# Cosine-similarity attention on one core: a five-bank score ring with exponentials of two and three banks, and the norms moved out of their PSUM bank

## The chip, the cores and the metric

One core of a Trainium2 chip. The metric is the device time of one launch in microseconds (us). The kernel before takes 189.99 us (median of 3 runs, 189.53 to 190.36).

## The reference

Q, K and V are [8, 12, 512, 64] in f32, tau is 0.1.

```python
Q_norm = Q / (np.linalg.norm(Q, axis=-1, keepdims=True) + 1e-10)
K_norm = K / (np.linalg.norm(K, axis=-1, keepdims=True) + 1e-10)
scores = np.einsum('bhqd,bhkd->bhqk', Q_norm, K_norm) / tau
weights = np.exp(scores - np.max(scores, axis=-1, keepdims=True))
weights = weights / (np.sum(weights, axis=-1, keepdims=True) + 1e-10)
return np.einsum('bhqk,bhkd->bhqd', weights, V).astype(np.float32)
```

There are 96 heads. For each, 512 x 512 exponentials are taken. The kernel leaves out the maximum: a cosine over tau lies between -10 and 10.

## The kernel before

**The work.** Two heads make a pair; there are 48 pairs, s = 0 to 47. All five engines run in order, each through its own list, and the lists are written out by hand in `ORDER` (numbers of operations in the order in which they are added). A step waits on semaphores for what it needs (`needs`), so a step whose input is late holds up all that stands behind it on its engine. The steps of one pair, with their names in the code, engines and lines:

- Q, K and V arrive by DMA (SP's queue). `SQ`: POOL squares Q and K together (L350).
- `SSQ`: for K, eight matmuls with the identity on PE add up the squares to eight columns a row, in columns 320 to 383 of an output bank `ops` (L367); `RED`: DVE adds up the rest (L375). For Q, DVE reduces the squares itself (L379).
- `NEW`: one over the root of the sums for a group of pairs (single pairs at first, then twos, from pair 20 on fours), eight or nine short DVE steps, each of which needs the one before it (L404 to L413).
- `SCL`: Q is scaled by DVE, K by POOL, in nine pairs by DVE (L437). `TR`: eight transposes on PE (L443), `EVA`: DVE copies them to `qt` (L451), a ring of four pairs.
- `SCO`: scores, 512 keys by 512 queries of a head; a chunk c is 128 keys of both heads, two matmuls of 512 columns into two PSUM banks (L550). `EXP`: ACT takes the exponential of the chunk, 1024 columns, to `et` (L566), a ring of five pairs.
- `PV`: for each head (h = 0 or 1) 16 matmuls of 65 columns on output bank `ops` h (L583); column 65 of each holds the sum of the weights. `RCP` (L594) and `NRM` (L596): DVE divides, and SP stores.

**PSUM** has eight banks: four for the scores (`scps`: chunk after chunk takes banks 0 and 1, then 2 and 3, in turn), two for the outputs (`ops0`, `ops1`), one for the transposes (`tps`), one for the norms (`nps`: the sums of squares, the Newton steps' product and the finished factors). A score chunk can be written when the exponential two chunks earlier has read its banks:

```python
used = [("EXP", 0, 2 * c, 1)] if turn < NT + 2 else exps(*chunks[turn - 2])
P.add(("SCO", s, c), "pe", "sco", T0 + 0.9 * c, used + [("EVA", s)], sco)
```

A `PV` of one output bank can start when `NRM` of the pair before has read that bank (`bank_free`).

**Around the loop.** Pair 0 has its own head (`head0`), with `FILL` matmuls on PE that compute nothing used. In pair 43 one chunk's exponential is made by DVE and POOL with a polynomial (`OFF`). The last pair ends in pieces (`last`).

Of the kernel before, what the change touches and what calls it, by code (L numbers as in the profile page):

```python
# [10 lines left out]
class Op:  # L11
    def __init__(self, key, eng, kind, due, needs, emit, slot=None):
# [3 lines left out]
        self.gate = None  # L16
# [4 lines left out]
class Program:  # L21


    def __init__(self, nc):
        self.nc, self.ops, self.list = nc, {}, []
# [18 lines left out]
    def run(self):  # L44
# [68 lines left out]
def bass_cosine_similarity_attention_kernel(  # L113
# [26 lines left out]
    et = [sb(f"et{i}", [128, NT, 2, SEQ], bf16) for i in range(R_ET)]  # L140
# [13 lines left out]
    sc_ps = nc.alloc_psum_tensor("scps", [128, 4, SEQ], f32)  # L154
# [4 lines left out]
    n_ps = nc.alloc_psum_tensor("nps", [128, R_X, 160], f32)  # L159
# [70 lines left out]
    for s in range(NP):  # L230
        for h in range(2):
            bank_free[s, h] = before[h]
            before[h] = [("NRM", s, h)] + ([("RED",) + attached[s, h]] if (s, h) in attached else [])

# [75 lines left out]
    def pair(s):  # L310
# [47 lines left out]
        x2 = (xs[g][:, 0 : 2 * m] if acts else n_ps[:, g % R_X, 0 : 2 * m]).rearrange("p (w x) -> p w x", w=2)  # L358
# [26 lines left out]
        rkd = n_ps[:, g % R_X, 128 + m : 128 + 2 * m] if acts else tg[:, m : 2 * m]  # L385
        on_dve = [i for i in range(first[g], first[g] + sizes[g]) if i in K_ON_DVE]
# [16 lines left out]
        elif s == first[g]:  # L403
# [13 lines left out]
            if on_dve:  # L417
                steps.append(up(tg[:, m : 2 * m], m, 2 * m))
            for k, step in enumerate(steps):
                needs = [("NEW", g, min(k, 6) - 1 if k < 8 else 7)] if k else reds + (free[1] if K_ON_DVE else [])  # L420
                if k == 0 and g == R_X:
                    needs += [("NRMS", 0, w, h) for w in range(2) for h in range(2)]
                if 6 <= k < 8:
                    needs += free[k - 6]
                P.add(("NEW", g, k), "dve", "new", TF - 4.9 - slack(s, M_NEW) + (M_STEP * (k - 7) if s > 8 else 0.23 * k), needs, step)

        if s in off_of:
            P.add(("UNIT", s), "dve", "new", TF - 3.0, [("NEW", g, 6)], lambda e: e.tensor_scalar(
                out=rq_g[:, c8 : c8 + 8], in0=rq_g[:, c8 : c8 + 8], scalar1=UNIT * inv_tau / math.log(2.0), scalar2=1.0,
                op0=ALU.mult, op1=ALU.mult))  # L430
        for w in range(2):
# [3 lines left out]
            P.add(("SCL", s, w), "dve" if dve else "pool", "sclq" if dve else "sclk", T0 - (2.85 if w and not dve else 2.55) - slack(s, M_SCL),  # L435
# [3 lines left out]
                      in0=qk[iq][:, w].rearrange("p h (t d) -> p h t d", t=NT), in1=r, op=ALU.mult))  # L439

# [15 lines left out]
    def scos(s):  # L456
        if s < 0:
            return []
        if s in off_of:
            return [("SCO", s, c) if c != off_of[s] else ("SCX", s, c - c) for c in range(NT)] + [("SCX", s, 1)]  # L460
        return [("SCO", s, c) for c in range(NT)] if s else [("SCO", 0, c, h) for c in range(NT) for h in range(2)]
# [4 lines left out]
    def exps(s, c):  # L466
# [6 lines left out]
        return [("Y", s, last_step(s, c)) if (s, c) in OFF else ("EXP", s, c)]  # L473
# [46 lines left out]
    def rest(s):  # L520
# [3 lines left out]
        for c in range(NT):  # L524
# [20 lines left out]
            turn = chunks.index((s, c))  # L545
            b = turn % 2

            def sco(e, c=c, b=b):
                for h in range(2):
                    last = e.matmul(  # L550
                        out=sc_ps[:, 2 * b + h, :], lhsT=qt[iqt][64 * h : 64 * h + 64, 1, c, :],
                        rhs=qt[iqt][64 * h : 64 * h + 64, 0, :, :], start=True, stop=True)
                return last

            used = [("EXP", 0, 2 * c, 1)] if turn < NT + 2 else exps(*chunks[turn - 2])
            P.add(("SCO", s, c), "pe", "sco", T0 + 0.9 * c, used + [("EVA", s)], sco)
            if last_pair and c == NT - 1:
# [90 lines left out]
UNIT = 128.0  # L648
# [167 lines left out]
```

## Time and profile before

| | |
|---|---|
| runs | 189.99 us median of 3, 189.53 to 190.36 |
| profiled execution | 190.25 us, of which the span from the first to the last instruction is 188.4 us |
| granted TensorE clock | 0.998 |
| busy share of the span | PE 93%, DVE 91%, ACT 96%, POOL 86% |
| instructions | PE 2714, DVE 552, ACT 213, POOL 150 |

How to read it: the profile is one execution. A busy time is the union of an engine's instructions, so overlapping ones count once; the mean of one instruction can therefore be longer than the step from one to the next. Idle time is put down to what ended it. The chain is followed back from the last instruction to what released each piece.

### The profile page before, as it was taken

Reading aid. Unit: us, or ns where it says so; the run is one execution under the profiler, and the core shown is the slowest. Engines: PE = TensorE matmul, PEld = TensorE weight load, DVE = VectorE, ACT = ScalarE, POOL = GpSimd, SP = SyncE. Lnnn points to the kernel's source line nnn. Section 1 sums busy time; section 2 is a strip of 40 time slices with the busy share of each in tenths; the row PEclk is TensorE's granted clock in tenths of the full one; section 3 lists DMA queues with packets and bytes.
Section 4 is the critical chain, followed back from the end, with each engine's and each line's share of the span. In section 5 each row is a group of like instructions: output and inputs, shape, how many; then the busy total and the mean of one; then the engine's idle time right before and its main releaser. Section 6 shows DMA issues by size and latency. Waiting matters only on the chain.

```text
span 188.4 us, 6686 instructions
## 1 busy us (share of the span) xinstructions
PE 174.7 (93%) x2714; PEld 108.8 (58%) x2714; DVE 170.5 (91%) x552; ACT 181.8 (96%) x213; POOL 162.1 (86%) x150
## 2 busy tenths in 40 slices
PE   7998998999999999999989999999989999999993
PEld 2555664666566566566656666666655555565662
DVE  2789999999999999999999998999999999998663
ACT  4799999999999999999999999999999999999993
POOL 5799999999999999999999999899999990594500
PEclk9999999999999999999999999999999999999999
DMA  5999999999999699999999869999470800038058
GB/s 164 348 353 351 349 350 282 294 377 378 379 366 356 188 293 347 377 381 361 366 373 354 285 187 336 380 361 349 123 234 5 278 6 0 3 120 273 2 179 270
DMA packets 52446, 50.76 MB, mean 269 GB/s; under 512 B 3136, under 2 KB 52416, under 8 KB 52416
## 3 DMA queue, kind: packets, MB, share of 16 engines
q1 hardware_dynamic: 51984, 50.02, 80.4%
q8 instruction: 21, 0.34, 0.7%
q10 hardware_dynamic: 432, 0.33, 0.5%
q14 instruction: 9, 0.07, 0.1%
HBM read 37.75 MB, written 12.58 MB: 267 GB/s over the span
## 4 chain that ended last, share of the span: by engine, by line
ACT 92%; PE 5%; DVE 1%; issue 0%; POOL 0%; POOLq 0%
ACT et L566 90%; PE ops L195 2%; PE ops L198 1%; DVE qn L437 1%; ACT et L542 1%; PE scps L533 1%; ACT et L561 0%; PE ops L281 0%; ACT ob L627 0%; PE ops L367 0%; DVE qt L292 0%; DVE ob L631 0%; PE tps L443 0%; PE scps L550 0%; PE tps L281 0%
## 5 line engine op out<-in xcount | busy, mean ns | idle before, releaser
L566 ACT ACTIVATE et<-scps 128x1024 bf16<-128x1024 f32 x186 | 170.6, 1203 | 0.0
L350 POOL TENSOR_TENSOR sq<-qk 128x1024 bf16<-128x1024 f32 x44 | 82.7, 1894 | 0.3 <-DMA qk<-in_Q_dram 0.3
L550 PE MATMUL scps<-qt 64*128 64x512 bf16 x374 | 73.0, 387 | 8.9 <-ACT et L566 6.4
L583 PE MATMUL ops<-vb,et 128*128 128x65 bf16 x1504 | 75.7, 194 | 0.0
L583 PEld LDWEIGHTS ops<-vb,et 128*128 128x128 bf16 x1504 | 56.7, 98 | 29.2 <-issue 18.8
L437 POOL TENSOR_TENSOR qn<-qk,rk 128x512 bf16<-128x512 f32 x38 | 39.2, 1043 | 1.9 <-DVE rk L409 1.5
L596 DVE TENSOR_TENSOR ob<-ops,rd 128x256 f32<-128x256 f32 x94 | 38.9, 418 | 0.8
L437 DVE TENSOR_TENSOR qn<-qk,nps 128x512 bf16<-128x512 f32 x56 | 37.0, 678 | 0.5 <-ACT nps L396 0.5
L550 PEld LDWEIGHTS scps<-qt 64*128 64x128 bf16 x374 | 18.1, 93 | 27.8 <-ACT et L566 17.9
L443 PE MATMUL tps<-ident,qn 128*128 128x128 bf16 x376 | 33.9, 220 | 0.1
L451 DVE COPY qt<-tps 128x1024 bf16<-128x1024 bf16 x47 | 32.1, 684 | 1.4 <-PE tps L443 1.2
L571 POOL TENSOR_SCALAR vb<-vf 128x512 bf16<-128x512 f32 x48 | 29.4, 627 | 2.6 <-DVE et L499 2.6
L379 DVE TENSOR_REDUCE nps<-sq 128x8 f32<-128x512 bf16 x46 | 31.2, 682 | 0.0
L443 PEld LDWEIGHTS tps<-ident,qn 128*128 128x128 bf16 x376 | 21.6, 98 | 9.4 <-issue 6.1
L594 DVE RECIPROCAL rd<-ops 128x4 f32<-128x4 f32 x94 | 16.0, 175 | 5.3 <-PE ops L583 4.3
L367 PE MATMUL ops<-sq,ident 128*128 128x64 bf16 x384 | 18.8, 193 | 0.0
L367 PEld LDWEIGHTS ops<-sq,ident 128*128 128x128 bf16 x384 | 14.3, 98 | 3.4 <-issue 2.2
L375 DVE TENSOR_REDUCE nps<-ops 128x8 f32<-128x64 f32 x46 | 10.0, 219 | 0.7 <-PE ops L367 0.4
L499 POOL TENSOR_TENSOR xz<-xz 128x1024 f32<-128x1024 f32 x1 | 1.9, 1892 | 6.6 <-DVE xz L494 6.6
L405 DVE SCALAR_TENSOR_TENSOR nps<-nps,ys 128x32 f32<-128x32 f32 (+2 forms) x34 | 7.0, 207 | 0.4
L404 DVE TENSOR_TENSOR nps<-nps,ys 128x32 f32<-128x32 f32 (+2 forms) x34 | 7.0, 205 | 0.4
L344 POOL TENSOR_TENSOR sq<-qk 128x512 bf16<-128x512 f32 (+1 forms) x5 | 4.6, 954 | 0.3 <-DMA qk<-in_K_dram 0.2
(67 smaller groups left out, 63.5 us busy)
## 6 DMA issues: line engine op xcount, KB each, us to landing
vf<-in_V_dram SPq DMA_DIRECT2D x48, 256.0 KB, 5.9
qk<-in_Q_dram SPq DMA_DIRECT2D x47, 256.0 KB, 6.1
qk<-in_K_dram SPq DMA_DIRECT2D x47, 256.0 KB, 6.1
out_dram<-ob SPq DMA_DIRECT2D x47, 256.0 KB, 5.4
qk<-in_Q_dram SPq DMA_DIRECT2D x2, 128.0 KB, 2.6
qk<-in_K_dram ACTq DMA_DIRECT2D x2, 128.0 KB, 2.8
out_dram<-ob SPq DMA_DIRECT2D x1, 128.0 KB, 2.0
out_dram<-ob SPq DMA_DIRECT2D x1, 64.0 KB, 1.8
```

Source lines behind the costliest of these rows:

```text
L350: lambda e: e.tensor_tensor(out=sqf, in0=data, in1=data, op=ALU.mult))
L367: last = e.matmul(out=o_ps[bank][:, 320:384], lhsT=ident[:, :], rhs=sq[iqs][:, 8 * w : 8 * w + 8, 8 * k : 8 * k + 8], start=(k == 0), stop ...
L379: lambda e, w=w, dst=dst: e.tensor_reduce(out=dst, in_=sq[iqs][:, 8 * w : 8 * w + 8, :], axis=AX.X, op=ALU.add))
L437: lambda e, w=w, r=r: e.tensor_tensor(out=qn[iqn][:, w].rearrange("p t h d -> p h t d"), in0=qk[iq][:, w].rearrange("p h (t d) -> p h t d" ...
L443: last = e.transpose(t_ps[:, w, t, :], qn[iqn][:, w, t].rearrange("p h d -> p (h d)"), ident[:, :])
L451: lambda e: e.tensor_copy(out=qt[iqt][:, :, :, :].rearrange("p w t x -> p (w t x)"), in_=t_ps[:, :, :, :].rearrange("p w t x -> p (w t x)")))
L550: last = e.matmul(out=sc_ps[:, 2 * b + h, :], lhsT=qt[iqt][64 * h : 64 * h + 64, 1, c, :], rhs=qt[iqt][64 * h : 64 * h + 64, 0, :, :], sta ...
L566: lambda e, c=c, b=b: e.activation(out=et[iet][:, c, :, :], in_=sc_ps[:, 2 * b : 2 * b + 2, :], func=ACT.Exp, scale=math.log(2.0) / UNIT i ...
L571: lambda e: e.tensor_scalar(out=vb[:, iq, :, :, 0:DIM].rearrange("p c h d -> p h c d"), in0=vf[iv][:, :, :].rearrange("p h (c d) -> p h c ...
L583: last = e.matmul(out=o_ps[h][:, 65 * t : 65 * t + 65], lhsT=et[iet][:, c, h, 128 * t : 128 * t + 128], rhs=vb[:, iq, c, h, :], start=(c = ...
L594: lambda e, h=h, grid=grid: e.reciprocal(out=rd[io][:, h, :], in_=grid[:, :, DIM]))
L596: lambda e, h=h, grid=grid: e.tensor_tensor(out=ob[io][:, h], in0=grid[:, :, 0:DIM], in1=rd[io][:, h, :].unsqueeze(2).to_broadcast([128, N ...
```

## The change

From pair 12 on (`WIDE`) the norms leave their PSUM bank and that bank becomes a fifth bank of `scps`. Score units (one bank: one head of one chunk) are taken two at a time into banks 0 and 1, then three at a time into banks 2, 3 and 4, in turn, and each group of units has one exponential, of 1024 or 1536 columns. `et` becomes one tile, so that such a group may run over a chunk's end or a pair's end; where the ring of `et` wraps, at pair 43 and before the last chunk the groups are cut. The list of ACT then has 103 exponentials of 1024 columns, 55 of 1536 and one of 512, where there were 186 of 1024; the columns are the same 190,464. DVE has 552 instructions as before.

The sums of squares of those pairs go to SBUF (`xn`), the Newton product to SBUF (`ys`), and the running root and the finished factors to columns 384 and up of an output bank, `ops0` or `ops1` by the group's number. `run()` therefore adds waits: a group's first Newton step waits for a `RCP` on that bank, and each first `PV` of a bank waits for the last DVE step on that bank's norm columns that stands ahead of that `PV`'s `RCP` in DVE's list. For pairs under 12 the norms stay where they were (the bank has another name, so order rows call it `scps`). A first triple that takes the bank waits for the last scalings that read it. `PV` now waits for the exponentials of its own head alone.

All lists in `ORDER` are written anew, the head's too. In the rows below, names are as in the code, numbers behind a name are the buffer; a row with `x7` is seven like instructions.

PE at the start of the program; before, `ops1<-warm_in` up to 512 columns are warm-up and fills, `ops0<-ident,qn0` are transposes of pair 0's K, `tps<-ident,qn0` of its Q:

```order
L195 MATMUL ops1<-warm_in,ident 128x512 x7
L198 MATMUL ops1<-warm_in,ident 128x384
L198 MATMUL ops1<-warm_in,ident 128x128
L198 MATMUL ops1<-warm_in,ident 128x192
L198 MATMUL ops1<-warm_in,ident 128x384
L281 MATMUL ops0<-ident,qn0 64x128 [waits s_act]
L281 MATMUL ops0<-ident,qn0 64x128 x3
L198 MATMUL ops1<-warm_in,ident 128x192
L281 MATMUL tps<-ident,qn0 64x128 [waits s_dve]
L281 MATMUL tps<-ident,qn0 64x128 x3
```

and now:

```order
L203 MATMUL ops1<-warm_in,ident 128x512 x7
L206 MATMUL ops1<-warm_in,ident 128x256
L206 MATMUL ops1<-warm_in,ident 128x192
L353 MATMUL ops0<-ident,qn0 64x128 [waits s_act]
L353 MATMUL ops0<-ident,qn0 64x128 x3
L353 MATMUL tps<-ident,qn0 64x128 [waits s_dve]
L353 MATMUL tps<-ident,qn0 64x128 x3
L206 MATMUL ops1<-warm_in,ident 128x384 x2
L206 MATMUL ops1<-warm_in,ident 128x128
```

Fills of 1280 columns stood ahead of the transposes of Q, and now 448 stand there; the rest comes behind.

PE while it makes the scores of pairs 18 and 19 (`scps<-qt2`, `qt3`); `ops0<-vb,et2` is the first `PV` of pair 17, `ops0<-sq0` an `SSQ`, `ops1<-vb,et1` `PV` of pair 16. Before:

```order
L550 MATMUL scps<-qt2 128x512 [waits s_act]
L550 MATMUL scps<-qt2 128x512
L443 MATMUL tps<-ident,qn3 128x128 [waits s_dve]
L443 MATMUL tps<-ident,qn3 128x128 x3
L583 MATMUL ops0<-vb,et2 128x65 [waits s_pool,s_dve]
L583 MATMUL ops0<-vb,et2 128x65 x3
L550 MATMUL scps<-qt2 128x512 [waits s_act]
L550 MATMUL scps<-qt2 128x512
L583 MATMUL ops0<-vb,et2 128x65 x12
L367 MATMUL ops0<-sq0,ident 128x64 x8
L550 MATMUL scps<-qt3 128x512 [waits s_dve,s_act]
L550 MATMUL scps<-qt3 128x512
```

and now, with the same `PV` of pair 17 and the same `SSQ`:

```order
L286 MATMUL scps<-qt2 128x512 [waits s_act]
L286 MATMUL scps<-qt2 128x512 x2
L658 MATMUL ops0<-vb,et 128x65 [waits s_dve]
L658 MATMUL ops0<-vb,et 128x65 x15
L440 MATMUL ops0<-sq0,ident 128x64 [waits s_pool]
L440 MATMUL ops0<-sq0,ident 128x64 x7
L286 MATMUL scps<-qt2 128x512 [waits s_act]
L286 MATMUL scps<-qt2 128x512
L658 MATMUL ops1<-vb,et 128x65 [waits s_dve]
L658 MATMUL ops1<-vb,et 128x65 x7
L286 MATMUL scps<-qt3 128x512 [waits s_act]
L286 MATMUL scps<-qt3 128x512 x2
```

Scores come as three banks and two in turn, and all 16 `PV` matmuls of the head and the eight of `SSQ` stand in one piece between a triple and a double.

DVE at the norms of pairs 20 to 23, while pairs 15 to 17 are divided (`rd` 7, 0 and 1 belong to pairs 15, 16 and 17). Before:

```order
L594 RECIPROCAL rd0<-ops0 128x4 [waits s_pe]
L375 TENSOR_REDUCE nps<-ops0 128x8
L413 TENSOR_SCALAR ys0<-nps 128x64 [waits s_dve]
L404 TENSOR_TENSOR nps<-nps,ys0 128x64 [waits s_dve]
L596 TENSOR_TENSOR ob0<-ops0,rd0 128x256 [waits d_out0]
L405 SCALAR_TENSOR_TENSOR nps<-nps,ys0 128x64 [waits s_dve]
L409 SCALAR_TENSOR_TENSOR ys0<-nps,ys0 128x64 [waits s_dve]
L594 RECIPROCAL rd7<-ops1 128x4 [waits s_pe]
L404 TENSOR_TENSOR nps<-nps,ys0 128x64 [waits s_dve]
L451 COPY qt3<-tps 128x1024 [waits s_pe]
```

and now:

```order
L490 TENSOR_SCALAR ops0<-xn0 128x64 [waits s_dve]
L481 TENSOR_TENSOR ys0<-xn0,ops0 128x64 [waits s_dve]
L482 SCALAR_TENSOR_TENSOR ys0<-ys0,ops0 128x64 [waits s_dve]
L673 TENSOR_TENSOR ob0<-ops0,rd0 128x256 [waits d_out0]
L486 SCALAR_TENSOR_TENSOR ops0<-ys0,ops0 128x64 [waits s_dve]
L671 RECIPROCAL rd7<-ops1 128x4 [waits s_pe]
L481 TENSOR_TENSOR ys0<-xn0,ops0 128x64 [waits s_dve]
L482 SCALAR_TENSOR_TENSOR ys0<-ys0,ops0 128x64 [waits s_dve]
L536 COPY qt3<-tps 128x1024
L673 TENSOR_TENSOR ob7<-ops1,rd7 128x256
L671 RECIPROCAL rd1<-ops0 128x4 [waits s_pe]
L486 SCALAR_TENSOR_TENSOR rk0<-ys0,ops0 128x32 [waits s_dve]
```

The Newton steps now work in `ops0`. The `PV` of pair 17 on `ops0` waited for `ob0<-ops0` alone; it now waits for the second `L482`, and the `RCP` that needs it (`rd1<-ops0`) stands two DVE instructions behind that.

The diff, cut to its core:

```diff
+        behind = {}
+        for o in order["dve"]:
+            if o.bank is not None:
+                behind[o.bank] = o.key
+            if o.key[0] == "RCP" and o.key[2] in behind:
+                self.first_value[o.key[1:]].needs.insert(0, behind.pop(o.key[2]))
...
-    et = [sb(f"et{i}", [128, NT, 2, SEQ], bf16) for i in range(R_ET)]
+    et_all = sb("et", [128, R_ET * NT * 2, SEQ], bf16)
...
-    sc_ps = nc.alloc_psum_tensor("scps", [128, 4, SEQ], f32)
+    sc_ps = nc.alloc_psum_tensor("scps", [128, 5, SEQ], f32)
+    xn = [sb(f"xn{i}", [128, 64], f32) for i in range(3)]
...
-    n_ps = nc.alloc_psum_tensor("nps", [128, R_X, 160], f32)
+    n_ps = sc_ps[:, 4, 0 : R_X * 160].rearrange("p (r x) -> p r x", r=R_X)
...
+    while units:
+        banks = [2, 3, 4] if side else [0, 1]
+        side = 1 - side
...
+        while len(take) < min(len(banks), len(units)):
+            v = units[len(take)]
+            if place(v) != place(take[-1]) + 1 or (v[0] in off_of) != (u[0] in off_of) or (v[:2] == (NP - 1, NT - 1)) != ends:
+                break
+            take.append(v)
...
+        plan.append((*keys, take, banks, sorted({bank_last[b] for b in banks if bank_last[b]}, key=str)))
...
+            for (s, c, h), b in zip(us, banks):
+                last = e.matmul(
+                    out=sc_ps[:, b, :], lhsT=qt[s % R_QT][64 * h : 64 * h + 64, 1, c, :],
+                    rhs=qt[s % R_QT][64 * h : 64 * h + 64, 0, :, :], start=True, stop=True)
...
+                   lambda e: e.activation(
+                       out=et_all[:, i : i + len(us), :], in_=sc_ps[:, banks[0] : banks[0] + len(us), :],
+                       func=ACT.Exp, scale=math.log(2.0) / UNIT if s in off_of else inv_tau))
...
+        inner = first[g] >= WIDE
...
+        if inner:
+            n_bank = o_ps[g % 2]
+            xg, tg, yg = xn[g % 3][:, 0 : 2 * m], ys[g % R_X][:, 0 : 2 * m], n_bank[:, 384 : 384 + 2 * m]
+            rq_g, rkd = n_bank[:, 448 : 448 + m], n_bank[:, 480 : 480 + m]
...
+                if k == 0 and inner:
+                    needs += [("RCP", 0, g % 2)] + (new(g - 2) if before2 else [])
...
+WIDE = 12
```

More of the change, by code (lines that the diff above doesn't have):

```diff
@@ new lines, in bass_cosine_similarity_attention_kernel @@
+    bank_last[4] = None
+    units = [(s, c, h) for s in range(WIDE, NP) for c in range(NT) for h in range(2) if (s, c) not in OFF]
+    place = lambda u: ((u[0] % R_ET) * NT + u[1]) * 2 + u[2]
+    side = 0
+    while units:
+        banks = [2, 3, 4] if side else [0, 1]
+        side = 1 - side
+        u = units[0]
+        take = [u]
+        ends = u[:2] == (NP - 1, NT - 1)
+        while len(take) < min(len(banks), len(units)):
+            v = units[len(take)]
+            if place(v) != place(take[-1]) + 1 or (v[0] in off_of) != (u[0] in off_of) or (v[:2] == (NP - 1, NT - 1)) != ends:
+                break
+            take.append(v)
+        units = units[len(take):]
+        banks = banks[: len(take)]
+        n = len(plan)
+        keys = (("SCO", NP - 1, NT - 1), None) if ends else (("SCG", n), ("EXG", n))
+        for v in take:
+            sc_of[v], ex_of[v] = keys
+        plan.append((*keys, take, banks, sorted({bank_last[b] for b in banks if bank_last[b]}, key=str)))
+        for b in banks:
+            bank_last[b] = keys[1]
@@ L544, in rest @@
                 continue
[L545 to L557, printed above, removed]
+            if s >= WIDE and not (last_pair and c == NT - 1):
+                continue
+            n = next(n for n, p in enumerate(plan) if (s, c, 0) in p[2])
+            banks = wide(n)
+            if s >= WIDE:
                 for k, (h, lo, hi) in enumerate(PIECES):
```

90 lines of the change are left out of this document (65 added, 25 removed), and 146 rows, old and new, of the table ORDER.

## The prediction

> **What bounds the kernel now.** I read the page's busy shares and chain first, to see which engine sets the end.
>
> ```profile
> PE 174.7 (93%) x2714; PEld 108.8 (58%) x2714; DVE 170.5 (91%) x552; ACT 181.8 (96%) x213; POOL 162.1 (86%) x150
> ACT 92%; PE 5%; DVE 1%; issue 0%; POOL 0%; POOLq 0%
> ```
>
> The chain in order of time says where ACT holds it:
>
> ```profile
> 13.32 170.20 ACT et L566 x186
> 183.53 0.89 ACT et L561
> ```
>
> From 13.32 to 183.53 us nothing but the 186 exponentials is on the chain: 170.20 / 186 = 0.915 us each (170.6 / 186 = 0.917 by busy time, below). Ahead of it lies a head of 13.3 us, behind it 4.9 us of the last pair. Next the windows, to see whether ACT ever waits and how much the others have left:
>
> ```profile
> core 0: us, PE busy (x) PEld busy (x) DVE busy (x) ACT busy (x) POOL busy (x), PEclk, DMA share, GB/s
> 50.00:70.00 20.00, 19.34 (x317) 12.28 (x313) 19.50 (x71) 20.00 (x24) 19.97 (x16) 1.00 0.94 308
> 70.00:90.00 20.00, 19.16 (x314) 12.02 (x310) 19.20 (x60) 20.00 (x23) 19.97 (x19) 1.00 1.08 365
> 90.00:110.00 20.00, 19.21 (x322) 12.59 (x320) 19.38 (x65) 20.00 (x23) 19.40 (x18) 1.00 0.94 316
> 110.00:130.00 20.00, 19.10 (x318) 12.32 (x316) 18.90 (x56) 20.00 (x23) 19.47 (x19) 1.00 1.05 347
> 130.00:150.00 20.00, 18.69 (x298) 11.73 (x296) 19.60 (x65) 20.00 (x23) 19.80 (x17) 1.00 0.55 174
> ```
>
> ACT never waits: 20.00 of 20.00 everywhere. But DVE is idle for only 0.50 + 0.80 + 0.62 + 1.10 + 0.40 = 3.42 us in these 100 us. A pair is four exponentials, 3.67 us, so DVE has 0.125 us to spare per pair. So the kernel is ACT's, with DVE close behind.
>
> **The change part by part. The exponentials.** What does one of them cost beside its columns? The groups by shape:
>
> ```profile
> L566 ACT ACTIVATE et<-scps 128x1024 bf16<-128x1024 f32 x186 | 170.6, 1203 | 0.0
> L542 ACT ACTIVATE et<-scps,xs 128x512 bf16<-128x512 f32 x4 | 2.5, 680 | 0.6 <-PE scps L533 0.6
> L538 ACT ACTIVATE et<-scps 128x1024 bf16<-128x1024 f32 x2 | 2.0, 1024 | 0.2 <-PE scps L533 0.2
> L342 ACT ACTIVATE sq<-qk 128x512 bf16<-128x512 f32 x1 | 0.6, 614 | 0.0
> L342 ACT ACTIVATE sq<-qk 128x256 bf16<-128x256 f32 x1 | 0.4, 400 | 0.0
> ```
>
> The two squares give the column rate: (614 - 400) / 256 = 0.836 ns, so 1024 columns are 0.856 us and the step of 0.917 us holds 0.061 us that does not depend on the columns. The columns stay 190,464; the instructions go from 186 to 103 + 55 + 1 = 159. 27 x 0.061 = **1.65 us less**, all of it on the path as long as ACT never waits. No row shows three banks read by one instruction, so this has bounds. An exponential after a wait takes 1.024 us (L538), 0.168 us over its columns: if all of that were saved it would be 27 x 0.168 = 4.5 us, but the step of 0.917 shows that 0.107 of it overlaps already. On the other side, the 0.061 could belong to the step from one bank to the next: 186 such steps before, 103 + 2 x 55 = 213 now, which is 1.65 us more. Against that speaks L542, one bank only, with more than 0.061 over its columns. I take 1.65.
>
> The Trainium skill (ScalarE: Activation LUTs, What ACT_TABLE_LOAD costs) gives 186 ns + 0.833 ns a column for such an instruction, and an overlap of about 93 ns between neighbours, so 93 ns are left of each; 27 x 0.093 would be 2.5 us. The trace's 0.917 us for 1024 columns is below the 0.946 us that follows from this, so I go by the row.
>
> **The five-bank ring.** Two timeline pieces show when scores must be ready:
>
> ```profile
> 93.78 2.15 ACT L566 ACTIVATE et<-scps 128x1024 bf16<-128x1024 f32 x2
> 95.06 0.39 PE L550 MATMUL scps<-qt 64*128 64x512 bf16 x2 [0.52 <-ACT et L566]
> ...
> 26.00 3.93 ACT L566 ACTIVATE et<-scps 128x1024 bf16<-128x1024 f32 x4
> 26.32 0.39 PE L550 MATMUL scps<-qt 64*128 64x512 bf16 x2 [0.20 <-ACT et L566]
> 26.64 0.67 PE L583 MATMUL ops<-vb,et 128*128 128x65 bf16 x16
> 27.14 0.40 PE L367 MATMUL ops<-sq,ident 128*128 128x64 bf16 x8
> 27.47 0.39 PE L550 MATMUL scps<-qt 64*128 64x512 bf16 x2
> ...
> 7.60 0.60 PE L533 MATMUL scps<-qt 64*128 64x512 bf16 x2
> ```
>
> The first two exponentials end at 95.93 and, one step of 0.917 earlier, at 95.01; PE stood waiting and began 0.05 us behind. In the second piece exponentials end at 29.93, 29.01, 28.10 and 27.18; the chunk at 27.47 came 0.29 us after its banks were free, was done at 27.86, 0.24 us ahead of 28.10, and ACT lost nothing. So a lead of 0.24 is harmless, and with it a pair of banks may start 0.29 us late. The pair's two matmuls run beside each other in 0.39. A third has to share rows with one of them; in L533 the second of two such ends 0.60 us after the first began, 0.21 later. A triple is thus done 0.05 + 0.60 = 0.65 us after its banks are free, while the exponential of 1024 runs 0.917: a lead of 0.27, so it may be late by 0.03 us only. A double has the 1536 exponential (1.28 + 0.06 = 1.34 us) beside it and may be late by 1.34 - 0.24 - 0.44 = 0.66.
>
> Does PE reach each triple in time? A cycle of five banks is 0.92 + 1.34 = 2.26 us.
>
> ```profile
> PEld scps L550 <- ACT et L566: 17.9, 61, 0.8
> PEld ops L583 <- DVE ob L596: 3.1, 12, 0.5
> ```
>
> Its weight loads for scores waited 17.9 us for ACT over 170 us, 0.24 us in 2.26. At pairs 17 to 19 (order above) PE has, behind the triple, 16 `PV` and 8 `SSQ`: the same work in the second piece takes 26.64 to 27.47, 0.83 us. With the triple itself (0.32 for two, from 26.32 to 26.64, and 0.21 for the third) PE is at the double 0.05 + 0.53 + 0.83 = 1.41 after the triple's banks were free, the double's banks having been free since 0.92: 0.49 late of 0.66, so it fits. Then a double (0.32) and eight `PV` and it is at the next triple by about 2.0 of 2.26. So the lists work if inputs are on time. PE's waits for DVE, 3.1 us in 12 places up to 0.5, pass on to ACT where they stand ahead of a triple. Nothing if none do; all 55 triples late like the chunk at 27.47 would be 55 x (0.29 - 0.05 - 0.03) = 11.6 us. The rows are nearer to the first end, since PE has 0.24 a cycle to catch up. A triple that runs into the next pair also needs `EVA` up to two banks earlier:
>
> ```profile
> 96.06 0.69 DVE L451 COPY qt<-tps 128x1024 bf16<-128x1024 bf16 x1
> 97.10 0.39 PE L550 MATMUL scps<-qt 64*128 64x512 bf16 x2
> ```
>
> Here the copy ends 0.35 us ahead of its first use, less than a bank's 0.46; a stall for that happens once, since it moves all that follows. For both I take **0.5 us more**.
>
> **The norms.** DVE keeps its 552 instructions, of like shapes, each still with one operand in PSUM; writing `xn` or `ys` where it wrote `nps` I cost at nothing, within 27 steps of 0.01 us either way. What is added is a wait. In `PV` of pair 17 the first matmul now waits for the second `L482`, and behind it on PE stand the other 15, `SSQ` and the double; the `RCP` that needs them has only these as cover:
>
> ```profile
> L596 DVE TENSOR_TENSOR ob<-ops,rd 128x256 f32<-128x256 f32 x94 | 38.9, 418 | 0.8
> L451 DVE COPY qt<-tps 128x1024 bf16<-128x1024 bf16 x47 | 32.1, 684 | 1.4 <-PE tps L443 1.2
> ```
>
> 1.10 us of cover against 0.50 + 0.40 = 0.90 for `PV` and `SSQ` by the second piece, and 0.05 for each of two handovers: DVE waits for 0 if PE stands ready, and up to 0.53 if a triple is ahead of it. Groups from pair 12 on are four of two and seven of four: 11, so 0 to 5.8 us of DVE's time at one such place each. ACT's gain takes 1.65 / 36 = 0.046 us per pair from DVE's 0.125, and 0.079 x 36 = 2.8 us stay as cover. I take it that they do.
>
> The Trainium skill (PSUM — Partial Sum Buffer, PSUM bank collisions raise a hardware error) says that PSUM must be guarded by bank, since two engines on different columns of one bank collide too; it speaks against norms in an output bank, and is why these waits can't be left out. No run here shows a collision.
>
> **The head.** These rows lie on its way:
>
> ```profile
> 4.76 0.40 ACT L247 ACTIVATE qn<-qk 128x256 bf16<-128x256 f32 x1
> 5.25 0.41 DVE L270 TENSOR_TENSOR qn<-qk,scps 128x256 bf16<-128x256 f32 x1
> 6.68 0.41 PE L281 MATMUL tps<-ident,qn 128*64 128x128 bf16 x4
> 6.78 4.76 POOL L344 TENSOR_TENSOR sq<-qk 128x256 bf16<-128x256 f32 x5 [0.18 <-DMA qk<-in_K_dram]
> 8.24 1.27 ACT L542 ACTIVATE et<-scps,xs 128x512 bf16<-128x512 f32 x2 [0.58 <-PE scps L533]
> 12.06 0.68 DVE L451 COPY qt<-tps 128x1024 bf16<-128x1024 bf16 x1
> ```
>
> Q is scaled by 5.66, yet its transposes begin at 6.68: fills stand ahead, and most now come behind. That could bring the first exponential forward from 8.24 to about 7.7, where ACT ends its squares. But POOL starts pair 1's squares when K lands, at 6.78, which no list moves, and `EVA` of pair 1 ends at 12.74 on a DVE that is full from there on. Between -0.5 and +0.2, which is a late Q scaling, I take **-0.2 us**.
>
> **Sum.** 190.25 (the profiled execution: span 188.4, 1.85 around it) - 1.65 + 0.5 - 0.2 = 188.9. That execution lies 0.26 above the median of 189.99, so the time is **188.6 us**; with the waits at 0 and the head at -0.5 it is 187.8, with them at 1.2 it is 189.3.
>
> **The rivals.** *The triples eat it.* PE is late for a triple in most cycles by 0.03 us more than it may be; 55 x 0.03 = 1.65 repays all. For it: the margin of 0.03; against: 17.9 us of waiting. About 189.8, between 189.2 and 190.6; chance 0.20.
>
> *The output banks bind DVE and PE (slower).* Two places for each of 11 groups in which DVE waits 0.3 us for a `PV` that waited for DVE: 6.6 - 2.8 = 3.8 us more on a DVE that then sets the pace, 188.9 - 0.5 + 3.8 - 0.26 = 191.9. It begins to tell at 2.8 / 11 = 0.25 us per group and makes the kernel slower than before by 0.5% at 0.51. For it: DVE's 97% in the windows; against: the 0.15 us of spare cover above. Chance 0.14.
>
> *More is saved per instruction*: the column rate comes from squares read from SBUF; if columns from PSUM take 0.805 ns, 1024 of them are 0.824 us, and the fixed part is 0.093 us: 188.6 - 27 x 0.032 = 187.7, chance 0.06. It is also what the Trainium skill's page (ScalarE: Activation LUTs, What ACT_TABLE_LOAD costs) would leave of each.
>
> *The bank step costs, not the instruction*: +1.65 in place of -1.65, 191.9; chance 0.03. Then the change would not do what it says.
>
> **How the numbers follow.** 0.5%, 0.95 us, is about what a measurement of this kernel can tell from no change: faster is below 189.04, slower above 190.94. My forecast has 0.57, of which 0.10 lies above 189.04. Faster: 0.47 + 0.06 + 0.02 of the late triples = 0.55. Slower: 0.12 of the second rival, 0.03, and 0.03 of triples that are later still = 0.18. No change: 0.27. The range goes from 187.5 (more saved per instruction) to 191.3, into the second rival; left out are most of that one and the bank step, under 0.2.
>
> **What would show it.** Right: 103 exponentials a step of 0.917 apart and 55 of 1.34, ACT busy 20.00 of 20.00 in the windows from 60 us on, and idle DVE near 2%. Wrong: a group of exponentials with idle time put down to PE (triples), or to PE that waited for DVE's norm lines L481 to L490 (banks); a step of 1.40 for 1536 columns (bank step); a first exponential of pair 1 later than 13.3 (head).

## The result and the profile after

The changed kernel takes 188.77 us (median of 5 runs, 188.52 to 189.14), the kernel before on the same chip 189.99 us (189.51 to 190.36): a ratio of 0.994, with a 95% interval of 0.9915 to 0.9964. The profiled execution took 188.81 us, with a span of 187.0 us, where it was 190.25 and 188.4.

First the page's busy shares and the chain's shares by engine, of the kernel after:

```profile
PE 174.6 (93%) x2714; PEld 106.2 (57%) x2714; DVE 169.5 (91%) x552; ACT 180.1 (96%) x186; POOL 161.8 (87%) x150
ACT 92%; DMA 3%; PE 2%; DVE 1%; issue 0%; SPq 0%
```

ACT has 27 instructions and 1.7 us of busy time less, and it still holds 92% of the chain. The chain in order of time (start, length, what) shows where it holds it, and where not:

```profile
13.20 154.88 ACT et L302 x146
...
168.12 0.62 PE scps L286 x3
...
168.76 13.29 ACT et L302 x12
```

The exponentials now end at 182.05, 1.48 us earlier than 183.53, after a start that is 0.12 earlier; and for the first time there is a place, at 168.1, where ACT had to wait for scores. The groups of ACT by shape (count, then busy time and mean ns, then idle time before):

```profile
L302 ACT ACTIVATE et<-scps 128x1024 bf16<-128x1024 f32 x103 | 105.4, 1111 | 0.1
L302 ACT ACTIVATE et<-scps 128x1536 bf16<-128x1536 f32 x55 | 85.0, 1545 | 0.2 <-PE scps L286 0.2
```

Three DVE groups of the norms, after:

```profile
L521 DVE TENSOR_TENSOR qn<-qk,ops 128x512 bf16<-128x512 f32 x41 | 27.0, 674 | 0.0
L481 DVE TENSOR_TENSOR ys<-xn,ops 128x64 f32<-128x64 f32 x14 | 3.1, 219 | 0.3
L490 DVE TENSOR_SCALAR ops<-xn 128x64 int32<-128x64 int32 x7 | 1.6, 224 | 0.0
```

and the groups that do the same in the kernel before:

```profile
L437 DVE TENSOR_TENSOR qn<-qk,nps 128x512 bf16<-128x512 f32 x56 | 37.0, 678 | 0.5 <-ACT nps L396 0.5
L404 DVE TENSOR_TENSOR nps<-nps,ys 128x64 f32<-128x64 f32 x14 | 3.2, 227 | 0.2
L413 DVE TENSOR_SCALAR ys<-nps 128x64 int32<-128x64 int32 x7 | 1.6, 225 | 0.1
```

The means of ACT's rows (1111 and 1545 ns) are longer than a step, because each instruction begins in the record before its forerunner ends. So I took steps from end to end in the single records of the trace: 0.917 us for each of the 102 steps of 1024 columns, 1.343 us for those of 1536. That is 0.8326 ns a column and 0.064 us that belongs to the instruction. The same overlap hides short gaps from every view of idle time; only the difference between a step and its nominal length (0.064 us and its columns) shows them. By that count the kernel after has two gaps, of 0.31 us at the place above and of 0.02 us.

Next the windows (length; busy time and count of PE, PEld, DVE, ACT, POOL; granted clock, DMA share, GB/s):

```profile
50.00:70.00 20.00, 19.24 (x318) 11.87 (x317) 19.54 (x71) 20.00 (x20) 20.00 (x16) 1.00 1.01 335
70.00:90.00 20.00, 19.41 (x320) 11.83 (x316) 19.15 (x62) 20.00 (x18) 20.00 (x19) 1.00 0.95 315
90.00:110.00 20.00, 19.29 (x321) 12.23 (x321) 18.93 (x60) 20.00 (x19) 20.00 (x19) 1.00 1.00 322
110.00:130.00 20.00, 19.12 (x301) 11.45 (x300) 19.08 (x56) 20.00 (x19) 19.31 (x17) 1.00 0.95 326
130.00:150.00 20.00, 18.68 (x299) 11.30 (x297) 19.48 (x64) 20.00 (x19) 18.61 (x19) 1.00 0.68 209
```

ACT is at 20.00 as before. DVE is idle for 3.82 us of the 100, where it was 3.42: the new lists took nothing from it. POOL is at 20.00 of 20.00 in three windows; it was at 19.97 in two of them before. The waits (total us, times, longest):

```profile
PEld scps L286 <- ACT et L302: 13.8, 49, 0.8
DVE rd L671 <- PE ops L658: 3.7, 8, 1.5
```

PE still stands waiting for ACT's banks, 13.8 us of it against 17.9. DVE's divisions (`rd`) wait for a `PV` in 8 places in the whole program, 3.7 us, where it was 11 places and 4.3 us. PE's weight loads for `PV` wait for the norm lines L481, L482 and L486 in eight places, 2.8 us together and 0.4 at most, and in the ten us ahead of the gap of 0.02 and the five ahead of the other there is none of these.

**Where the 1.44 us came from.** 27 instructions of 0.064 us are 1.73 less; the two gaps give 0.335 back; the head is 0.12 shorter, the stretch behind the last exponential 0.10 longer: -1.73 + 0.335 - 0.12 + 0.10 = -1.41. The span is 1.39 us shorter; the other 0.05 lie outside it.

**The gap.** The timeline of pair 43, where the group is cut (start, length, what; in brackets the idle time ahead and what ended it):

```profile
165.86 0.60 PE L286 MATMUL scps<-qt 64*128 64x512 bf16 x3
167.22 0.39 PE L286 MATMUL scps<-qt 64*128 64x512 bf16 x1
168.12 0.11 PEld L286 LDWEIGHTS scps<-qt 64*128 64x128 bf16 x3 [0.24 <-ACT et L302]
168.12 0.60 PE L286 MATMUL scps<-qt 64*128 64x512 bf16 x3
168.76 1.45 ACT L302 ACTIVATE et<-scps 128x1536 bf16<-128x1536 f32 x1 [0.20 <-PE scps L286]
```

A triple, a single bank and another triple follow each other. The single's exponential lasts 0.49 us; the next triple, started 0.05 us after its banks were free, needs 0.60 and cannot be done beside that. Every other triple has at least 0.917 us beside it.

### The profile page after: what moved, and what is told of

Same layout as the page of the kernel before. It is cut to its first block, busy times and chain, and to the rows that moved or that the text cites. A ratio compares the mean times of both kernels' runs of the same rounds, so it can differ in the third digit from the quotient of the medians.

```text
span 187.0 us, 6660 instructions
## 1 busy us (share of the span) xinstructions
PE 174.6 (93%) x2714; PEld 106.2 (57%) x2714; DVE 169.5 (91%) x552; ACT 180.1 (96%) x186; POOL 161.8 (87%) x150
## 4 chain that ended last, share of the span: by engine, by line
ACT 92%; DMA 3%; PE 2%; DVE 1%; issue 0%; SPq 0%
ACT et L302 90%; DMA qk<-in_Q_dram 3%; DVE qn L521 1%; ACT et L630 1%; PE scps L286 1%; SPq L393 0%; ACT et L641 0%; ACT sq L414 0%; PE ops L440 0%; PE scps L621 0%; ACT ob L706 0%; DVE ob L710 0%; PE tps L528 0%; PE ops L689 0%; DVE rd L702 0%
## 5 line engine op out<-in xcount | busy, mean ns | idle before, releaser
L302 ACT ACTIVATE et<-scps 128x1024 bf16<-128x1024 f32 (+1 forms) x159 | 169.0, 1259 | 0.3 <-PE scps L286 0.2
L286 PE MATMUL scps<-qt 64*128 64x512 bf16 x374 | 74.0, 385 | 6.7 <-ACT et L302 4.6
L658 PEld LDWEIGHTS ops<-vb,et 128*128 128x128 bf16 x1504 | 55.6, 98 | 32.1 <-issue 16.5
L658 PE MATMUL ops<-vb,et 128*128 128x65 bf16 x1504 | 72.0, 194 | 0.3 <-DVE ob L673 0.3
L286 PEld LDWEIGHTS scps<-qt 64*128 64x128 bf16 x374 | 16.3, 93 | 22.1 <-ACT et L302 13.8
L521 DVE TENSOR_TENSOR qn<-qk,ops 128x512 bf16<-128x512 f32 x41 | 27.0, 674 | 0.0
L452 DVE TENSOR_REDUCE xn<-sq 128x8 f32<-128x512 bf16 x38 | 25.2, 674 | 0.2
L521 DVE TENSOR_TENSOR qn<-qk,scps 128x512 bf16<-128x512 f32 x15 | 9.9, 676 | 0.1
L448 DVE TENSOR_REDUCE xn<-ops 128x8 f32<-128x64 f32 x34 | 7.0, 210 | 0.5 <-PE ops L440 0.5
L452 DVE TENSOR_REDUCE scps<-sq 128x8 f32<-128x512 bf16 x8 | 5.4, 684 | 0.1
```

The lines of the kernel that those rows point to most:

```text
L286: last = e.matmul(out=sc_ps[:, b, :], lhsT=qt[s % R_QT][64 * h : 64 * h + 64, 1, c, :], rhs=qt[s % R_QT][64 * h : 64 * h + 64, 0, :, :], s ...
L302: lambda e: e.activation(out=et_all[:, i : i + len(us), :], in_=sc_ps[:, banks[0] : banks[0] + len(us), :], func=ACT.Exp, scale=math.log(2 ...
L452: lambda e, w=w, dst=dst: e.tensor_reduce(out=dst, in_=sq[iqs][:, 8 * w : 8 * w + 8, :], axis=AX.X, op=ALU.add))
L521: lambda e, w=w, r=r: e.tensor_tensor(out=qn[iqn][:, w].rearrange("p t h d -> p h t d"), in0=qk[iq][:, w].rearrange("p h (t d) -> p h t d" ...
L658: last = e.matmul(out=o_ps[h][:, 65 * t : 65 * t + 65], lhsT=et[iet][:, c, h, 128 * t : 128 * t + 128], rhs=vb[:, iq, c, h, :], start=(c = ...
```

## The experiments

Two theories go in. **The first**, the prediction's: each instruction on ACT costs 0.06 us beside its columns, a triple is just in time, and behind ACT stands DVE. **The rivals**: the fixed time belongs to the step between banks; the norms in the output banks were free, or were not; another engine stands behind ACT.

**e1_cut43: the one gap.** The group at pair 43 is cut as two and two, so that no single remains.

```diff
         u = units[0]
+        if u[0] in off_of:
+            banks = banks[:2]
```

> Pair 43's six score banks as three doubles in place of a double, a triple and a single. Theory (ACT sets the pace, and the one gap of 0.31 us on ACT comes from a triple of 0.65 us standing beside an exponential of 512 columns, 0.49 us): the number of exponentials stays 159, the gap goes, 188.77 - 0.31 = 188.46 us, and no gap above 0.03 us is left on ACT. Rival (the gap only takes up a wait for DVE or POOL that lies behind pair 43): the gap moves to another place, 188.8 us.

188.51 us (188.16 to 189.65), ratio to before 0.9915 (0.9882 to 0.9948). The chain of this kernel has no break left:

```profile
12.80 168.51 ACT et L304 x159
```

159 instructions in one piece, and no step over its nominal length. **f1_after_again** and **f2_cut43_again** repeat the pair on one chip, with the kernel after and the kernel of e1 unchanged.

> The changed kernel once more, beside the version with pair 43's scores as three doubles on the same chip: a ratio to before of 0.9915 to 0.9964, and the same gap of 0.31 us on ACT in pair 43.

> Pair 43's scores as three doubles, beside the changed kernel on the same chip. Theory: 0.31 us less than that one, no gap on ACT. Rival (the gap moves): the same time.

188.73 us (188.33 to 188.85; ratio 0.9923, 0.9906 to 0.9939) and 188.45 us (188.02 to 188.86; ratio 0.9911, 0.9892 to 0.9929). In the traces the gap of 0.311 us is there in the first, in the same place, and gone in the second; the first exponential to the last takes 169.20 and 168.90 us. The medians differ by 0.28, as that says, but the runs overlap: the gap and its end are shown by the trace, the time alone would not prove them. By its medians this version is the fastest of all that compute the whole reference.

**e2_split: is it the instruction or the bank?** A triple's exponential is issued as one of 1024 and one of 512 columns: the same columns and banks, 55 instructions more, and 55 fewer steps from bank to bank inside an instruction.

```diff
-                   lambda e: e.activation(
-                       out=et_all[:, i : i + len(us), :], in_=sc_ps[:, banks[0] : banks[0] + len(us), :],
-                       func=ACT.Exp, scale=math.log(2.0) / UNIT if s in off_of else inv_tau))
+                   lambda e: [e.activation(
+                       out=et_all[:, i + lo : i + hi, :], in_=sc_ps[:, banks[0] + lo : banks[0] + hi, :],
+                       func=ACT.Exp, scale=math.log(2.0) / UNIT if s in off_of else inv_tau)
+                       for lo, hi in ((0, 2), (2, 3))[: len(us) - 1 or 1] for hi in (min(hi, len(us)),)][-1])
```

> Each exponential of 1536 columns as two instructions, of 1024 and 512; scores, lists and waits as they are. Theory (0.064 us of an instruction do not depend on its columns): 55 more instructions, 188.77 + 55 x 0.064 = 192.3 us, and steps of 0.917 and 0.491 us in place of 1.343. Rival (the cost lies in the step from one bank to the next): 55 such steps fewer, 188.77 - 3.5 = 185.3, or no change where they overlap. Rival (DVE or PE sets the pace): below 190, since ACT's added time falls into time in which it would wait.

192.12 us (191.9 to 193.13), ratio 1.0102 (1.0066 to 1.0138). From the first exponential's record to the last it is 172.69 us, 3.46 more than in after: 0.063 us for each of the 55. The fixed time is the instruction's. Does a step from bank to bank cost anything beside it? In f3 (below) a triple's exponential has 128 columns fewer and the same three banks, and where it doesn't wait its step is 1.236 us for 1.343: 0.107 us, or 0.84 ns a column, which is the whole rate. So a step between banks costs nothing that can be seen, and that rival falls. By an estimate from the figures of the Trainium skill (ScalarE: Activation LUTs, What ACT_TABLE_LOAD costs), 186 ns less about 93 ns of overlap, 0.093 us of each would be left; here it is 0.064.

**e3_late512 and f4_late256: how late may a triple be?** Each triple begins with a matmul more, on its first bank, which the real one then overwrites: 512 columns in e3, 256 in f4.

```diff
+            if len(us) == 3:
+                s, c, h = us[0]
+                e.matmul(
+                    out=sc_ps[:, banks[0], 0:512], lhsT=qt[s % R_QT][64 * h : 64 * h + 64, 1, c, :],
+                    rhs=qt[s % R_QT][64 * h : 64 * h + 64, 0, 0:4, :], start=True, stop=True)
```

> A matmul of 512 columns that nothing uses ahead of each triple of scores, behind the triple's wait: the triple is done 0.21 us later. Theory (a triple is done 0.26 us ahead of the end of the exponential beside it, and about 0.145 of that is needed): 0.26 - 0.21 = 0.05 us of lead, so 0.1 us of gap on ACT at each of 54 triples, 188.77 + 5.3 = 194.1 us; PE, which waits 13.8 us for ACT, has the 11.7 us. Rival (a lead of 0.05 us is enough): 188.8 to 189.5 us.

> As the matmul of 512 columns ahead of each triple, but of 256: the triple is done 0.107 us later, its lead falls from 0.26 to 0.15 us. Theory (0.143 is needed): no gap at the triples that start on time; late ones lose what they are late, up to 16 of 55 by 0.1, so 188.8 to 190.5 us. If the lead needed were 0.24, as was allowed for: 0.09 at each of 54 triples, 193.5 us.

e3: 196.57 us (196.48 to 197.14), ratio 1.0332 (1.0299 to 1.0365), 2.5 us over the 194.1 that was expected. f4: 191.01 us (190.72 to 191.21), ratio 1.0047 (1.0027 to 1.0067), 0.5 over the upper end. One triple of each, e3 first; the row of L287 is the added matmul, L291 the three real ones:

```profile
64.86 0.39 PE L287 MATMUL scps<-qt 64*128 64x512 bf16 x1
64.86 0.81 PE L291 MATMUL scps<-qt 64*128 64x512 bf16 x3
```

```profile
64.50 0.28 PE L287 MATMUL scps<-qt 64*128 64x256 bf16 x1
64.51 0.70 PE L291 MATMUL scps<-qt 64*128 64x512 bf16 x3
```

Triples now end 0.82 and 0.71 us after their start, where it was 0.60. By the single records, a triple that PE starts as soon as its banks are free is done 0.042 us before the exponential beside it ends in e3, and a gap of 0.101 to 0.102 us follows nearly each time; in f4 it is 0.148 us before, and the gap is 0.001. Both say the same: scores must be complete about **0.143 us** before the forerunner ends. In the kernel after they are 0.26 us ahead, so a triple may start 0.12 us late.

What e3's theory missed are the others. The added matmuls have filled PE (19.5 to 19.9 us of 20 in its windows), so 13 triples also start 0.09 to 0.14 us later than the others and have gaps of 0.19 to 0.24 us; with 0.53 at the single of pair 43 all gaps of e3 are 7.46 us, where 5.3 were expected on top of after's 0.335. f4's gaps are 1.64 us, 0.42 of them at the single. Its span is 1.9 us over f1's: 1.3 in the exponentials, 0.4 less in the head, and 1.0 more behind the last exponential, where PE still has `PV` to do; what makes up that 1.0 I have not settled.

**e4_norms_in_sbuf, g1_root_in_sbuf, g2_factors_in_sbuf: what the place of the norms is worth.** Are the free columns of the output banks needed, or only a nuisance with their waits? In e4 product, running root and factors all lie in SBUF, and the waits on the output banks go with them.

```diff
-            n_bank = o_ps[g % 2]
-            xg, tg, yg = xn[g % 3][:, 0 : 2 * m], ys[g % R_X][:, 0 : 2 * m], n_bank[:, 384 : 384 + 2 * m]
-            rq_g, rkd = n_bank[:, 448 : 448 + m], n_bank[:, 480 : 480 + m]
+            n_sb = nsb[g % 2]
+            xg, tg, yg = xn[g % 3][:, 0 : 2 * m], ys[g % R_X][:, 0 : 2 * m], n_sb[:, 0 : 2 * m]
+            rq_g, rkd = n_sb[:, 64 : 64 + m], n_sb[:, 96 : 96 + m]
...
-                    needs += [("RCP", 0, g % 2)] + (new(g - 2) if before2 else [])
+                    needs += new(g - 2) if before2 else []
```

> The Newton steps' root and factors of the pairs from 12 on in SBUF in place of the output banks, and without the waits that the output banks need; lists as they are. Theory (ACT sets the pace and these waits fall into spare time): 188.8 us, within 0.3; the waits of the value matmuls for DVE's norm lines go. Rival (these waits cost): no more to win than the gaps on ACT, 0.33 us, plus what the head leaves; 188.4. Rival (steps with both operands in SBUF are slower for DVE or hinder POOL): above 189.3.

236.45 us (234.43 to 239.07), ratio 1.2387 (1.2337 to 1.2437): the theory missed by 48 us, and the rival had the direction, not the size. The groups of e4, the same as those shown of after (`warm_in` is the name of the reused SBUF tile):

```profile
L522 DVE TENSOR_TENSOR qn<-qk,warm_in 128x512 bf16<-128x512 f32 x41 | 47.8, 1180 | 0.0
L482 DVE TENSOR_TENSOR ys<-xn,warm_in 128x64 f32<-128x64 f32 x14 | 7.2, 515 | 0.3
L491 DVE TENSOR_SCALAR warm_in<-xn 128x64 int32<-128x64 int32 x7 | 7.0, 1001 | 0.0
```

Each scaling lasts 1.180 us and not 0.674, a step that reads two small tiles 0.515 and not 0.219, the first guess of the root 1.001 and not 0.224. DVE's busy time goes from 169.5 to 213.1 us, POOL's from 161.8 to 179.2; both waited inside their instructions. PE then waits for DVE, and ACT for PE:

```profile
PEld ops L659 <- DVE ob L674: 27.2, 23, 3.4
ACT et L303 <- PE scps L287: 42.7, 43, 4.1
```

Since e4 took waits away as well, g1 and g2 keep every wait and move one thing each: g1 the running root (line `xg, tg, yg` of the diff), g2 the finished factors (line `rq_g, rkd`).

> As the changed kernel with all its waits, but the running root of the Newton steps of the pairs from 12 on lies in SBUF; the finished factors stay in the output banks. Theory (a DVE instruction with no operand in PSUM is held up by POOL): these steps grow by about 23 us as they did with all norms in SBUF, the scalings stay at 0.674 us; DVE has 4 to spare, 205 to 210 us. Rival (the missing bank waits upset the order of the lists): 188.8 us, since the waits are all there.

> As the changed kernel with all its waits, but the finished factors lie in SBUF and the root stays in the output bank. Theory (held up by POOL): the 41 scalings take about 1.18 us in place of 0.674, 20.8 us more for DVE, the Newton steps stay; 203 to 208 us. Rival (the place of the factors does not matter): 188.8 us.

g1: 214.83 us (213.72 to 215.93), ratio 1.1283 (1.1138 to 1.1428). g2: 215.47 and 221.03 us in its two runs, which give no interval. Both cost more than expected: g1 5 us over the upper end, g2 7.5 in the shorter of its runs. g1's groups, and g2's:

```profile
L482 DVE TENSOR_TENSOR ys<-xn,warm_in 128x64 f32<-128x64 f32 x14 | 8.4, 604 | 0.3
L491 DVE TENSOR_SCALAR warm_in<-xn 128x64 int32<-128x64 int32 x7 | 6.7, 959 | 0.0
```

```profile
L522 DVE TENSOR_TENSOR qn<-qk,warm_in 128x512 bf16<-128x512 f32 x41 | 51.0, 1259 | 0.0
L491 DVE TENSOR_SCALAR ops<-xn 128x64 int32<-128x64 int32 x7 | 1.6, 224 | 0.0
```

What was moved is slow, what stayed in the bank is not. DVE's busy time is 21.9 us more in g1 and 23.3 in g2, together 45.2, e4's 43.6. So it is the place and not the waits. How an instruction is held up shows in a piece of g2's timeline:

```profile
95.30 1.89 POOL L422 TENSOR_TENSOR sq<-qk 128x1024 bf16<-128x1024 f32 x1
96.85 0.89 DVE L522 TENSOR_TENSOR qn<-qk,warm_in 128x512 bf16<-128x512 f32 x1
97.16 1.65 POOL L647 TENSOR_SCALAR vb<-vf 128x512 bf16<-128x512 f32 x2
```

and in the same stretch of after:

```profile
96.18 1.24 POOL L646 TENSOR_SCALAR vb<-vf 128x512 bf16<-128x512 f32 x2
96.88 0.66 DVE L521 TENSOR_TENSOR qn<-qk,ops 128x512 bf16<-128x512 f32 x1
```

In g2 the scaling ends at 97.74, 0.55 us after POOL's square has ended at 97.19, although it began at 96.85; and POOL's two casts behind it take 1.65 us together. In after the scaling lasts 0.66 us and the casts 1.24, side by side: with one operand in a PSUM bank neither sees the other. The single records say so throughout. In g2, 38 of the 41 scalings began while POOL worked; 36 of these ended 0.53 to 0.55 us after the POOL instruction that was running, whether they lasted 0.68 or 2.39 us, the two others 1.12 us after it, and the three that began beside an idle POOL took 0.69. In after 40 of 41 began while POOL worked, and all lasted 0.65 to 0.69. The Trainium skill (SBUF — State Buffer, SBUF: two separate sides) has this rule: DVE with two SBUF inputs, or in a mode that uses both its ports, and POOL share a pair of ports that one instruction holds to its end. The runs agree with it. Not every such instruction pays: `L487`, with both inputs in SBUF, stays at 0.21 us in e4 and g1 in its seven calls of 128x64. Beside none of these 14 calls was POOL at work. The shares of the 26 to 48 us that are hold-up, that are lost order behind it, and that are a lower granted clock (a mean of 0.911 in e4, 0.96 in g1, 0.952 in g2, for 1.00 in after), I cannot part.

**f3_short_triples and h1_short_squares: who stands behind ACT?** In f3, on top of e1, a triple's exponential takes 1408 of 1536 columns (54 x 128 columns less, 5.76 us); in h1, besides, POOL squares half of a pair's columns from pair 12 on.

```diff
-                       out=et_all[:, i : i + len(us), :], in_=sc_ps[:, banks[0] : banks[0] + len(us), :],
+                       out=et_all[:, i : i + len(us), :].rearrange("p u q -> p (u q)")[:, 0 : 512 * len(us) - 128 * (len(us) == 3)],
+                       in_=sc_ps[:, banks[0] : banks[0] + len(us), :].rearrange("p u q -> p (u q)")[:, 0 : 512 * len(us) - 128 * (len(us) == 3)],
...
-                  lambda e: e.tensor_tensor(out=sqf, in0=data, in1=data, op=ALU.mult))
+                  lambda e, n=512 if s >= WIDE else 1024: e.tensor_tensor(out=sqf[:, 0:n], in0=data[:, 0:n], in1=data[:, 0:n], op=ALU.mult))
```

> As the version with three doubles, but each exponential of a triple takes 1408 of its 1536 columns and leaves the last 128 out: 54 x 128 x 0.833 = 5.76 us less for ACT. If nothing but ACT set the pace, 188.46 - 5.76 = 182.7 us. Theory that DVE is close behind (idle 3.82 of the 100 us from 50 to 150, while ACT's cut in that stretch is 4.6): ACT now waits, DVE's idle share falls to 1% or less, 183.5 to 185.5. Rival (the bank waits bind DVE and PE already): above 186, with DVE still idle for 2 to 3% and waiting for value matmuls.

> As the run with short exponentials of triples (the last 128 columns of each left out), and from pair 12 on POOL squares 512 of the 1024 columns of a pair (K's squares are left out, stale ones are summed): 36 x 0.94 = 34 us less for POOL. Theory (in that run POOL set the pace from 60 to 114 us): 186.2 falls by 1.5 to 3 us, to 183.2 to 184.7, and POOL is off the chain. Rival (DVE or the bank waits set it): within 0.5 us of 186.2.

f3: 186.2 us (186.12 to 186.33), ratio 0.9793 (0.9775 to 0.9812). That is 2.25 us under f2, not 5.76, and a smaller gain than the theory that DVE stands next gave. Two windows and five pieces of the chain of f3:

```profile
70.00:90.00 20.00, 19.56 (x324) 12.17 (x323) 19.35 (x62) 19.66 (x19) 20.00 (x19) 1.00 0.92 307
90.00:110.00 20.00, 19.51 (x328) 12.14 (x325) 19.07 (x59) 19.80 (x19) 20.00 (x19) 1.00 1.03 338
```

```profile
63.77 1.85 POOL sq L425
74.69 3.70 POOL sq L425 x2
89.33 3.71 POOL sq L425 x2
...
113.04 1.86 POOL sq L425
114.92 1.28 DVE xn L455 x2
```

ACT has idle time at last, DVE too, POOL has none from 50 to 110 us, and from 62.7 to 114.9 us the chain runs over POOL, its squares above all. From there to about 160 us it runs mostly over DVE. By the time alone, and by DVE's 3.3 of 100 us of idle time, the rival that the bank waits bind DVE and PE would fit as well; h1 decides. It takes POOL's load off: 184.4 us (184.26 to 184.71), ratio 0.97 (0.9678 to 0.9722), 1.8 us under f3 and within what was expected. Its windows:

```profile
50.00:70.00 20.00, 19.54 (x328) 12.16 (x327) 19.62 (x72) 20.00 (x20) 13.73 (x16) 1.00 1.03 345
90.00:110.00 20.00, 19.86 (x331) 12.45 (x328) 19.63 (x61) 20.00 (x20) 16.19 (x20) 1.00 0.98 321
```

DVE's instructions last as long in h1 as in f3 (`qn` on `ops` 0.675 us in both), so it is POOL's own work that counted. So **POOL** stands first behind ACT, up to 115 us; behind it come DVE and PE, over which the chain of h1 runs. In the kernel before, POOL's windows of 19.97 from 50 to 90 us show no more to spare; that it would have been next there too was not tested. On which engine comes first, the theory of the prediction falls; in f3's later part it is DVE.

**h2_wide10: the convoy, where lists don't fit.** The wide ring begins at pair 10, on top of e1, with PE's list placed anew for it and DVE's order kept; ACT has 157 exponentials.

```diff
-WIDE = 12
+WIDE = 10
```

The new list of PE is not shown.

> The version with three doubles, with triples from pair 10 on and PE's list of pairs 10 to 14 placed anew by the share of ACT's columns: 157 exponentials in place of 159 and the norms of pairs 10 and 11 in an output bank. Theory (0.064 us each): 188.45 - 0.13 = 188.32 us if every triple there starts on time, and up to 0.1 us more for each that is late; rival (POOL sets the pace there): 188.45 or more.

195.64 us (194.32 to 195.82), ratio 1.0276 (1.0247 to 1.0304): a miss of 7.3 us. The norms of pairs 10 and 11 now lie in an output bank, and its first `PV` waits for their last step on DVE, which stands late in a list that was not made for that. The timeline of h2:

```profile
40.33 0.30 PE L660 MATMUL ops<-vb,et 128*128 128x65 bf16 x4 [2.03 <-DVE ops L488]
41.68 1.02 ACT L304 ACTIVATE et<-scps 128x1024 bf16<-128x1024 f32 x1 [1.99 <-PE scps L288]
43.10 0.69 DVE L538 COPY qt<-tps 128x1024 bf16<-128x1024 bf16 x1 [2.82 <-PE tps L530]
45.38 1.04 POOL L523 TENSOR_TENSOR qn<-qk,rk 128x512 bf16<-128x512 f32 x1 [2.75 <-DVE rk L488]
```

PE waits 2.03 us at that `PV`, and behind it on PE stand the scores; ACT waits 1.99 for them, DVE 2.82 for transposes, POOL 2.75 for a factor. From 40 to 50 us ACT is busy for 5.42 us:

```profile
40.00:50.00 10.00, 7.92 (x95) 5.29 (x96) 4.83 (x19) 5.42 (x6) 7.25 (x8) 0.71 1.09 378
```

ACT is idle for 4.6 us of these ten, the larger part of the miss. This is the prediction's slower rival at one place: a wait of 2.03 us where a list doesn't fit it. In the kernel after the lists keep clear of it.

## Why the prediction came out

It gave 188.6 us in a range of 187.5 to 191.3 and "faster" as the likeliest; 188.77 was measured, and the ratio's interval ends at 0.9964. By its steps:

- **The exponentials**, -1.65: 27 x 0.064 = -1.73 was measured. The fixed part, taken from two squares on ACT, was right to 0.003 us, and e2 shows that it belongs to the instruction. More saved per instruction (0.093) is refuted, by e2 too, and so is the bank step, by e2 and f3.
- **The five-bank ring**, part of +0.5: a triple was put at 0.65 us after its banks are free and is done at 0.66; its lead was put at 0.27 and is 0.26. The lead that ACT needs was only bounded, at 0.24; it is 0.143. So the margin was 0.12 us and not 0.03, and the rival in which the triples eat the gain stood on the wrong bound. PE was waiting at 51 of 55 triples, one was late enough to cost 0.02 us, and doubles that started up to 0.9 us late still kept a lead of 0.29 or more.
- The whole term was +0.5 and the gaps are +0.335, but the agreement is partly luck: 0.31 of it is the single bank at pair 43, which the prediction never costed, although 0.49 us of exponential beside 0.65 us of triple could have been worked out from its own rows. Stalls for DVE and for `EVA`, which it did cost, did not come.
- **The norms**, 0: DVE's rows are as before (0.674 us a scaling, steps within 0.01), its idle time 3.82 against 3.42, so the waits that were added cost nothing that shows. "Each still with one operand in PSUM" is not true of every row: the 38 reductions `xn<-sq` have none, and take 0.674 us where those into `nps` took 0.682. Of the scalings and Newton steps it is true, and there it carried more than it was given weight for: without it the same change costs 26 to 48 us (g1, g2, e4). That rival, an edit of a few words away, was not on the list.
- **The output banks bind DVE and PE**, the slower rival: not in this kernel: PE's waits for the norm lines reach 0.4 us and none passes on to ACT. In h2 it is real: at one place PE waits 2.03 us and DVE behind it 2.82, where the prediction took 0.3 for DVE.
- **"With DVE close behind"** is the step that failed. With ACT shortened, POOL holds the chain first (62.7 to 114.9 us of f3) and DVE only from there on, and halving POOL's squares is worth 1.8 us (h1). The step came from the windows, and the column beside it stood there as well: POOL at 19.97 of 20 from 50 to 90 us. The size of DVE's cover, 2.8 us, was never called upon, so the number did not suffer.
- **The head**, -0.2: -0.12 in this pair of profiles. But the same kernel's exponentials began at 13.20 in one execution and at 13.40 in another (f1), so a term of this size isn't resolved.

## What to carry to other kernels

When one engine is at 100%, a saving in its fixed cost per instruction comes through in full as long as each input is ready early enough before the forerunner ends; look for the shortest instruction in the new order, because the longest input stands beside it sooner or later. Look at every engine's column of the windows for the next one, and test it by taking work from the first. And before small operands are moved, ask what else reads the memory they go to: the place of a few columns decided over more time here than everything the change was made of.

## What the runs showed of the hardware

- On ACT, an exponential of n columns adds 0.064 us + 0.8326 ns a column to a full queue, over one, two or three PSUM banks alike (after, e2, f3). Its input must be complete 0.143 us before the forerunner's end; later costs the difference (0.101 for a lead of 0.042 in e3, 0.311 in after where the scores came 0.166 after that end).
- Two matmuls of 512 columns that lie on different 64 rows take 0.39 us together. A third, which must share rows with one of them, makes it 0.60, and a fourth 0.82 (e3).
- DVE instructions whose operands all lie in SBUF, next to a busy POOL: 128x512 scalings take a mean of 1.18 to 1.26 us for 0.674, a 128x64 `TENSOR_SCALAR` 0.96 to 1.00 for 0.224. A scaling that begins while POOL works ends 0.53 to 0.55 us after POOL's instruction (36 of 38 in g2). Reductions with their one input in SBUF (`xn<-sq`) do not pay: 0.67 us in all these kernels. In g2 and e4, with the scalings moved, POOL's busy time rises too, by 18 and 17 us; in g1 it does not (162.1).
- Where PE stood idle the granted clock fell: 0.71 in h2's window from 40 to 50 us, against 1.00 in the windows of after. How much of these kernels' time that is, no run parts.
